# Transposes of the merged branches and of the second norm's input by DMA, as 16-bit halves, in a hybrid decoder layer

## The chip, the cores and the metric

The kernel runs on one core of one Trainium2 chip. The metric is device time in microseconds (us). The time before is the median of three runs, 1434.75 us (1433.64 to 1435.78). The kernel is written with a tile framework: buffers come from pools that hand out a buffer again when its last reader is done, a scheduler orders the instructions of each engine, and operations wrapped in `tc.keep_in_program_order` stay in the order in which the program writes them.

## The reference, cut to what matters

One layer over a sequence of 256 tokens of width 2048, all in float32:

```
h = rmsnorm(x, g_mix)
proj = h @ w_in                          # q, k, v of 16 heads, and 3 x 2048 gates
gates = sigmoid(proj[..., 3*2048:])      # one gate per branch, token and channel
o_a, o_b, o_c = three kinds of causal attention (4, 6 and 6 heads of 128)
merged = gates[0]*(o_a @ w_branch[:512]) + gates[1]*(o_b @ w_branch[512:1280])
       + gates[2]*(o_c @ w_branch[1280:])
x = x + merged @ w_out                   # "x1" below
h2 = rmsnorm(x, g_ffn)
gu = h2 @ w_gu                           # 2048 -> 2 x 5632
x = x + (silu(gu[..., :5632]) * gu[..., 5632:]) @ w_down
```

## The kernel before, in words

Every product is made of float32 operands split in two parts: `split` lets ScalarE copy an operand into a rounded high part (`hi`, type fp32r), and VectorE subtract it to get the low part (`lo`). `product` then issues three matmuls, high by high, high by low and low by high. Weights arrive as 512 KB pieces `w_raw` (two blocks of 128 rows by 512 columns, 4 buffers) through SyncE's queue, and are split into `w_hi` and `w_lo` (5 buffers each).

The activations must have the channels on the partitions. What a projection leaves is the other way round: PSUM tiles of 128 tokens by 512 columns. `transpose4` therefore lets TensorE transpose four 128x128 blocks into a PSUM tile `tr`, from which the split reads.

Two stages matter here. In the **branch stage** (about 535 to 642 us in the profile) a loop runs over four chunks of 512 columns, and within it over three branches of 4, 6 and 6 blocks of 128 rows. Each branch's product is multiplied by its gates, which GpSimd's queue loads from `gate_mem`, and added up in `ms`, one tile for each half (t = 0, 1) of the tokens. `to_m` then transposes the merged chunk into `m`, split in high and low. In the **output stage** (about 642 to 733 us) a loop over four chunks multiplies `m` by `w_out`; `keep_x1` adds x, stores the sum as `x1`, lets ScalarE sum the squares, and `next_h` makes the chunk of the next projection's input: transposed, multiplied by the norm's gain `g2` (VectorE), split, and for chunks 0 and 1 combined further (`put_sums`).

Work that follows a chunk isn't done at once. It's a generator in the list `stages`, and `project` calls `advance(stages)` once per block of 128 rows of the next projection, so that transposes and splits fall between that projection's matmuls. `finish_stages` runs what is left of the list.

The small tiles of 2 KB a partition (`half_kb`) come from the pool `scratch`, which has 12 of them for everything: merged tiles, gates, x, squares, multiplied columns.

Of the kernel before, what the change touches and what calls it, by code (L numbers as in the profile page):

```python
# [8 lines left out]

F32 = mybir.dt.float32  # L10
F32R = mybir.dt.float32r
AF = mybir.ActivationFunctionType
ALU = mybir.AluOpType
AX = mybir.AxisListType
# [3 lines left out]
P = 128  # L18
D = 2048
S = 256  # L20
NT = S // P
# [7 lines left out]
NB = 512  # L29
# [25 lines left out]
def hybrid_block(ctx: ExitStack, tc: tile.TileContext, x, g_mix, w_in, q_gain, k_gain, w_branch, w_out,  # L55
                 g_ffn, w_gu, w_down, rel_bias, onehot, extra, out):
    nc = tc.nc
# [21 lines left out]
    def pool(stack, name, side, bufs=1):  # L79
        return stack.enter_context(tc.tile_pool(name=name, bufs=bufs, side=side, reuse_waits="tile"))  # L80
# [5 lines left out]
    scratch = pool(ctx, "scratch", "right", 12)  # L86
    gx = pool(pgx, "gx", "right", 2)

    def half_kb(dt=F32):

        return scratch.tile([P, NB], dt, name="sc")
# [13 lines left out]
    def split(hi, lo, src, pin=False):  # L105
        for op in nc.scalar.copy(hi, src), nc.vector.tensor_sub(lo, src, hi.bitcast(F32)):  # L106
            if pin:
                tc.keep_in_program_order(op)

    def raw_weights(w, row0, c, col0):  # L110
        raw = wpool.tile([P, 2, NB], F32, name="w_raw", bufs=4)
        src = w[row0 + c * P: row0 + (c + 2) * P, col0: col0 + NB].rearrange("(k p) n -> p k n", p=P)
        return raw, nc.sync.dma_start(raw, src)

    def weights(w, row0, k0, nk, col0, there=()):

        for i, c in enumerate(range(k0, nk, 2)):
            raw = there[i] if i < len(there) else raw_weights(w, row0, c, col0)[0]
            hi = wpool.tile([P, 2, NB], F32R, name="w_hi")
            lo = wpool.tile([P, 2, NB], F32R, name="w_lo")  # L120
            split(hi, lo, raw)
# [4 lines left out]
    stages, slow_stages = [], []  # L126

    def advance(queue):
        while queue:
            try:  # L130
                next(queue[0])
                return
            except StopIteration:
                queue.pop(0)

    def finish_stages(queue):
        while queue:
            advance(queue)
# [25 lines left out]
    def rsqrt_mean(dst, ss, n, cols):  # L164
# [3 lines left out]
        y = small.tile([P, cols], F32, name=f"rs_y{cols}")  # L168
        nc.scalar.activation(y, v, AF.Ln)
        nc.scalar.activation(y, y, AF.Exp, scale=-0.5)  # L170
        t = small.tile([P, cols], F32, name=f"rs_t{cols}")
# [6 lines left out]
    def transpose4(src):  # L178

        pt = tr.tile([P, 4, P], F32, name="tr")  # L180
        for i in range(4):
            nc.tensor.transpose(pt[:, i, :], src[:, i * P:(i + 1) * P], ident)
        return pt


    class Columns:


        def __init__(self, pl, name, nk):
            self.hi, self.lo = (pl.tile([P, nk, S], F32R, name=f"{name}_{n}") for n in ("hi", "lo"))  # L190

# [20 lines left out]
    class Sums:  # L212
# [8 lines left out]
        def place(self, pl, c):  # L221
            self.s[c] = [pl.tile([P, 4, S], F32R, name=f"{self.name}_s{n}{c}") for n in ("hi", "lo")]

# [14 lines left out]
    class Chunks(Sums):  # L238
# [9 lines left out]
        def place(self, pl, c):  # L248
            if c in self.wc:
                super().place(pl, c)  # L250
                self.t[c] = [[pl.tile(sh, F32R, name=f"{self.name}_{t}{n}{c}") for n in ("hi", "lo")]
                             for t, sh in enumerate(([P, 4, P], [P, 2, P]))]
            else:
                self.t[c] = [pl.tile([P, 4, S], F32R, name=f"{self.name}_{n}{c}") for n in ("hi", "lo")]

# [136 lines left out]
    hs = Both(p1, h, WC)  # L392
# [6 lines left out]
    def load_x(c, queue):  # L399
        xc = [half_kb() for _ in range(NT)]  # L400
        for t in range(NT):
            queue(xc[t], x[t * P:(t + 1) * P, c * NB:(c + 1) * NB])
        return xc

    def to_h(acts, src, c, t, g, by_scalar=False):

        pt = transpose4(src)
        tmp = half_kb().rearrange("p (k q) -> p k q", k=4)
        if by_scalar:
            for i in range(4):  # L410
                nc.scalar.activation(tmp[:, i], pt[:, i], AF.Copy, scale=g[:, 4 * c + i:4 * c + i + 1])
        else:
            nc.vector.tensor_mul(tmp, pt, g[:, 4 * c:4 * c + 4, None].to_broadcast([P, 4, P]))
        acts.put(c, t, tmp)
        return tmp

    def squares(xc, dst, c, pin=False):
        for t in range(NT):
            sq = nc.scalar.activation(half_kb(), xc[t], AF.Square, accum_out=dst[:, t, c:c + 1])
            if pin:  # L420
                tc.keep_in_program_order(sq)
# [4 lines left out]
    g2 = consts.tile([P, KT], F32, name="g2")  # L426
# [4 lines left out]
    xc = [half_kb() for _ in range(NT)]  # L431
# [74 lines left out]
    with tc.manual_schedule(engines={mybir.EngineType.PE, mybir.EngineType.DVE, mybir.EngineType.Activation}):  # L506
# [14 lines left out]
        low_high(0, 1)  # L521
        high_low(0, 1)
        turned = [transpose4(xs[1][0])]
        high_high(1, 0)
        high_high(1, 1)
# [7 lines left out]
        high_high(0, 2)  # L533
        low_high(0, 2)
        turned.append(transpose4(xs[1][1]))
        high_high(1, 2)
        low_high(1, 2)
# [89 lines left out]
    def stick_breaking(hl, qT, kT, v):  # L627
# [7 lines left out]
        l = pa.tile([P, n], F32, name="p", bufs=1)  # L635
        nc.scalar.activation(l, z[:, :n], AF.Abs)
        nc.scalar.activation(l, l, AF.Exp, scale=-1.0)
        nc.scalar.activation(l, l, AF.Ln, bias=1.0)
# [214 lines left out]
    m = Columns(pool(pm, "pm", "right"), "m", KT)  # L853

    def to_m(c, srcs):
        for t in range(NT):
            m.put(c, t, transpose4(srcs[t]))
            yield

    for c in range(4):  # L860
        ms = [half_kb() for _ in range(NT)]
        for b, (k0, nk) in enumerate(((0, H_A), (H_A, H_B), (H_A + H_B, H_C))):
            gt = [half_kb() for _ in range(NT)]
            for t in range(NT):
                nc.gpsimd.dma_start(gt[t], gate_mem[b, c, t])
            ps = project(o, k0, w_branch, k0 * P, nk, c * NB)
            for t in range(NT):
                if b == 0:
                    nc.vector.tensor_mul(ms[t], ps[t], gt[t])
                else:  # L870
                    nc.vector.tensor_mul(gt[t], ps[t], gt[t])
                    nc.vector.tensor_add(ms[t], ms[t], gt[t])
        stages.append(to_m(c, ms))
    finish_stages(stages)
    ph1.close()


    pe = pool(ctx, "pe", "left")
    h2 = Chunks(pool(h2_stack, "h2p", "left"), "h", KT // 4, WC)

    def next_h(c, xc):
        hs = []
        for t in range(NT):
            hs.append(to_h(h2, xc[t], c, t, g2))
            yield
        if c in WC:
            h2.put_sums(c, *hs)
            yield
# [3 lines left out]
    def keep_x1(c, ps, xc):  # L892
        for t in range(NT):
            nc.vector.tensor_add(xc[t], ps[t], xc[t])
            nc.gpsimd.dma_start(x1[t, :, c * NB:(c + 1) * NB], xc[t])
        squares(xc, ss2, c)
        stages.append(next_h(c, xc))

    gx = pool(h2_stack, "gx2", "left", 2)
    for c in range(4):  # L900
        xc = load_x(c, nc.gpsimd.dma_start)
        ps = project(m, 0, w_out, 0, KT, c * NB)
        if c == 3:
            ahead = begin_pair(h2, w_gu, 0, D_FF)
        keep_x1(c, ps, xc)
# [191 lines left out]
```

## Time and profile before

| | |
|---|---|
| median of three runs | 1434.75 us |
| the profiled execution's own time | 1433.64 us |
| its span | 1431.9 us |
| TensorE (PE) busy | 1421.7 us, 99% |
| VectorE (DVE) busy | 1196.0 us, 84% |
| ScalarE (ACT) busy | 882.0 us, 62% |
| HBM read and written | 292.65 MB and 16.27 MB, 216 GB/s over the span |
| granted TensorE clock | 1.0 throughout |

The span is the time between the first and the last instruction; the execution's own time has 1.7 us more around it. In a row of a group, "x" is the number of instructions, then come busy time and the mean duration of one, then the idle time of that engine just before them and what ended it. A row of a timeline gives start, duration, engine, line, operation, output and input tile; in brackets the engine's idle time before it and what released it. `PEld` is the loading of the stationary operand, which overlaps the matmuls.

### The profile page before, as it was taken

To read this page: it belongs to the slowest core of one execution; us is meant where nothing else is said; L and a number is where in the kernel's file an instruction comes from. 1 tells how busy PE (TensorE), PEld (TensorE's weight loads), DVE (VectorE), ACT (ScalarE), POOL (GpSimd) and SP (SyncE) were. 2 spreads that over 40 slices of the span, in tenths; PEclk is the share of its full clock that TensorE was granted. 3 is DMA by queue.
4 is the path that set the end of the run, shared out by engine and by line. 5 is a ranking of instruction groups with operands and counts; after the bars stand their busy time and mean duration, and the time that the engine had idled before them with its cause. 6 is when DMAs were issued, how large, how long until landed. Compare 5 with 4: busy or idle time off the path is not lost. (4 is left out here: it accounts for less than half of the span.)

```text
span 1431.9 us, 17773 instructions
## 1 busy us (share of the span) xinstructions
PE 1421.7 (99%) x6404; PEld 1172.1 (82%) x6404; DVE 1196.0 (84%) x1262; ACT 882.0 (62%) x1140; POOL 72.6 (5%) x133
## 2 busy tenths in 40 slices
PE   9999999999999999999999999999999999999998
PEld 7888888888788888888888888888888888788887
DVE  7888787857999886776689999999999998886775
ACT  7667876766766665444456666666666666554453
POOL 1000000000000002100100000000000010100000
PEclk9999999999999999999999999999999999999999
DMA  8763647465666758866786657666665666767552
GB/s 270 264 218 119 220 127 247 122 221 173 215 203 238 257 194 291 278 224 211 223 299 224 224 206 251 216 225 229 219 217 191 231 212 223 256 230 240 190 169 97
DMA packets 154472, 310.09 MB, mean 217 GB/s; under 512 B 10672, under 2 KB 12288, under 8 KB 154384
## 3 DMA queue, kind: packets, MB, share of 16 engines
q1 hardware_dynamic: 143200, 275.29, 57.1%
q0 software_dynamic: 10000, 32.62, 6.5%
q10 hardware_dynamic: 1184, 1.06, 0.2%
q8 instruction: 50, 0.82, 0.2%
q14 instruction: 38, 0.31, 0.1%
HBM read 292.65 MB, written 16.27 MB: 216 GB/s over the span
## 5 line engine op out<-in xcount | busy, mean ns | idle before, releaser
L106 DVE TENSOR_TENSOR w_lo<-w_raw,w_hi 128x1024 fp32r<-128x1024 f32 x334 | 406.0, 1221 | 91.1 <-ACT w_hi L106 87.5
L106 ACT CAST w_hi<-w_raw 128x1024 fp32r<-128x1024 f32 x334 | 349.0, 1052 | 166.1 <-PE qs L162 67.4
L106 ACT CAST w_hi<-g_raw 128x1024 fp32r<-128x1024 f32 x184 | 192.6, 1053 | 120.4 <-PE ps L162 39.4
L106 DVE TENSOR_TENSOR w_lo<-g_raw,w_hi 128x1024 fp32r<-128x1024 f32 x184 | 219.6, 1220 | 36.1 <-ACT w_hi L106 35.2
L106 ACT CAST w_hi<-u 128x1024 fp32r<-128x1024 f32 x138 | 144.9, 1053 | 136.1 <-DVE u L303 65.1
L106 DVE TENSOR_TENSOR w_lo<-u,w_hi 128x1024 fp32r<-128x1024 f32 x138 | 166.5, 1221 | 37.0 <-ACT w_hi L106 35.6
L161 PE MATMUL ps<-w_lo,h_hi 128*128 128x512 f32 x360 | 140.9, 392 | 0.0
L162 PE MATMUL ps<-w_hi,h_lo 128*128 128x512 f32 x360 | 140.5, 390 | 0.0
L160 PE MATMUL ps<-w_hi,h_hi 128*128 128x512 f32 x360 | 137.5, 393 | 0.0
L161 PE MATMUL qs<-w_lo,h_hi 128*128 128x512 f32 x332 | 130.0, 392 | 0.8 <-DVE w_lo L106 0.8
L162 PE MATMUL qs<-w_hi,h_lo 128*128 128x512 f32 x332 | 129.6, 390 | 0.0
L160 PE MATMUL qs<-w_hi,h_hi 128*128 128x512 f32 x332 | 126.7, 391 | 0.0
L303 DVE TENSOR_TENSOR u<-u,g_raw 128x1024 f32<-128x1024 f32 x80 | 94.4, 1218 | 0.0
L162 PEld LDWEIGHTS ps<-w_hi,h_lo 128*128 128x128 f32 x360 | 67.6, 188 | 14.0
L161 PEld LDWEIGHTS ps<-w_lo,h_hi 128*128 128x128 f32 x360 | 67.6, 188 | 13.7
L160 PEld LDWEIGHTS ps<-w_hi,h_hi 128*128 128x128 f32 x360 | 67.5, 188 | 13.7
L161 PEld LDWEIGHTS qs<-w_lo,h_hi 128*128 128x128 f32 x332 | 62.4, 188 | 13.9 <-DVE w_lo L106 1.2
L162 PEld LDWEIGHTS qs<-w_hi,h_lo 128*128 128x128 f32 x332 | 62.4, 188 | 13.4 <-issue 0.6
L160 PEld LDWEIGHTS qs<-w_hi,h_hi 128*128 128x128 f32 x332 | 62.3, 188 | 12.7
L314 DVE TENSOR_TENSOR u<-g_raw 128x1024 f32<-128x1024 f32 x40 | 48.8, 1219 | 21.0 <-DMA g_raw<-in_w_in 16.2
L160 PE MATMUL v<-w_hi,h_hi 128*128 128x512 f32 x120 | 47.5, 396 | 0.2 <-ACT w_hi L106 0.2
L161 PE MATMUL v<-w_lo,h_hi 128*128 128x512 f32 x120 | 47.1, 393 | 0.0
(397 smaller groups left out, 2935.2 us busy)
## 6 DMA issues: line engine op xcount, KB each, us to landing
w_raw<-in_w_in SPq DMA_DIRECT2D x118, 512.0 KB, 4.6
g_raw<-in_w_gu SPq DMA_DIRECT2D x88, 512.0 KB, 5.1
w_raw<-in_w_gu SPq DMA_DIRECT2D x88, 512.0 KB, 6.4
g_raw<-in_w_in SPq DMA_DIRECT2D x72, 512.0 KB, 5.8
w_raw<-in_w_down SPq DMA_DIRECT2D x64, 512.0 KB, 4.6
w_raw<-in_w_branch SPq DMA_DIRECT2D x32, 512.0 KB, 5.1
w_raw<-in_w_out SPq DMA_DIRECT2D x32, 512.0 KB, 4.7
g_raw<-in_w_down SPq DMA_DIRECT2D x24, 512.0 KB, 5.3
```

What stands on the lines that cost most here:

```text
L106: for op in nc.scalar.copy(hi, src), nc.vector.tensor_sub(lo, src, hi.bitcast(F32)):
L160: nc.tensor.matmul(ps, ah, wh, start=start, stop=False, **how)
L161: nc.tensor.matmul(ps, ah, wl, start=False, stop=False, **how)
L162: nc.tensor.matmul(ps, al, wh, start=False, stop=stop, **how)
L303: tc.keep_in_program_order(nc.vector.tensor_add(d, d, a))
L314: nc.vector.tensor_add(d, a, b)
```

## The change

Seven times, for the four merged chunks and for chunks 0, 1 and 2 of the second norm's input, TensorE's eight transposes of a chunk go. In their place `turn_out` lets ScalarE copy a tile of 128x512 float32 into two planes of 16-bit halves (all low halves, then all high halves, 128x1024 in all), and ScalarE's queue issues a DMA transpose, which turns the eight blocks of 128x128 halves. `turn_in` lets ScalarE copy the two planes back between each other, so that the float32 words stand again, now transposed, in a scratch tile. `to_m` spreads this over the steps of the next projection: two steps to split and issue, five empty steps, two steps to join and split into high and low. In `keep_x1` the two `turn_out` come at once, and `next_h` waits four steps before it joins; the gain is then multiplied from scratch tile to scratch tile. Chunk 3 of the second norm's input stays with TensorE. The call of `finish_stages` after the loop over merged chunks goes, so that the last chunk of `m` is made during the first projection of the output stage.

```diff
+    def turn_out(src):
+        halves = scratch.tile([P, 2, NB], U16, name="sc")
+        tc.keep_in_program_order(nc.scalar.copy(halves, src.bitcast(U16).rearrange("p (n b) -> p b n", b=2)))
+        turned = scratch.tile([P, 8, P], U16, name="sc")
+        tc.keep_in_program_order(nc.scalar.dma_start_transpose(turned, halves.rearrange("p b n -> p (b n)")))
+        return turned
+
+    def turn_in(turned):
+        dst = half_kb().rearrange("p (k q) -> p k q", k=4)
+        tc.keep_in_program_order(nc.scalar.copy(dst.bitcast(U16).rearrange("p k (q b) -> p b k q", b=2),
+                                                turned.rearrange("p (b k) q -> p b k q", b=2)))
+        return dst
...
     def to_m(c, srcs):
+        turned = []
         for t in range(NT):
-            m.put(c, t, transpose4(srcs[t]))
+            turned.append(turn_out(srcs[t]))
+            yield
+        for _ in range(5):
+            yield
+        for t in range(NT):
+            m.put(c, t, turn_in(turned[t]))
             yield
...
         stages.append(to_m(c, ms))
-    finish_stages(stages)
     ph1.close()
...
-    def next_h(c, xc):
+    def next_h(c, xc, turned):
         hs = []
+        if turned:
+            for _ in range(4):
+                yield
         for t in range(NT):
-            hs.append(to_h(h2, xc[t], c, t, g2))
+            if turned:
+                tmp = turn_in(turned[t])
+                nc.vector.tensor_mul(tmp, tmp, g2[:, 4 * c:4 * c + 4, None].to_broadcast([P, 4, P]))
+                h2.put(c, t, tmp)
+            else:
+                tmp = to_h(h2, xc[t], c, t, g2)
+            hs.append(tmp)
             yield
...
-        stages.append(next_h(c, xc))
+        stages.append(next_h(c, xc, [turn_out(xc[t]) for t in range(NT)] if c < 3 else None))
```

More of the change, by code (lines that the diff above doesn't have):

```diff
@@ L11 @@
 F32R = mybir.dt.float32r
+U16 = mybir.dt.uint16
 AF = mybir.ActivationFunctionType
```

## The prediction

> **What bounds the kernel now.** I read the summary of the page first, then busy time by stretch over the two stages that the change touches (the branch projections, about 535 to 642 us, and the output projection, about 642 to 733 us), then TensorE's and ScalarE's timelines there.
>
> ```profile
> span 1431.9 us, 17773 instructions
> PE 1421.7 (99%) x6404; PEld 1172.1 (82%) x6404; DVE 1196.0 (84%) x1262; ACT 882.0 (62%) x1140; POOL 72.6 (5%) x133
> ```
>
> ```profile
> core 0: us, PE busy (x) PEld busy (x) DVE busy (x) ACT busy (x) POOL busy (x), PEclk, DMA share, GB/s
> 575.00:595.00 20.00, 20.00 (x94) 16.66 (x93) 15.63 (x20) 9.05 (x10) 3.20 (x6) 1.00 0.81 273
> 595.00:615.00 20.00, 20.00 (x94) 16.66 (x93) 15.59 (x19) 8.52 (x10) 3.22 (x6) 1.00 0.80 259
> 680.00:700.00 20.00, 20.00 (x94) 16.63 (x94) 13.80 (x17) 10.00 (x15) 2.16 (x4) 1.00 0.75 237
> 735.00:760.00 25.00, 24.84 (x113) 20.02 (x112) 23.54 (x33) 18.15 (x24) 0.00 (x0) 1.00 0.82 287
> ```
>
> TensorE has no gap in these stages, at the full granted clock; ScalarE (ACT) is busy 43 to 50% of them, VectorE (DVE) 69 to 78%, the DMA engines 75 to 81%. So in these stages a TensorE instruction that disappears is worth its slot, as long as no other engine becomes late. After 735 us PE still misses only 0.16 us of 25.
>
> The slot of a group of eight transposes is read from TensorE's timeline, and the pace of its matmuls from ScalarE's, where TensorE releases each cast of a pair of weight tiles:
>
> ```profile
> start us, us, engine line op out<-in xcount [idle before <-releaser]
> 579.94 0.39 PE L161 MATMUL qs<-w_lo,o_hi 128*128 128x512 f32 x1
> 580.16 0.39 PE L162 MATMUL qs<-w_hi,o_lo 128*128 128x512 f32 x1
> 580.40 1.03 PE L182 MATMUL tr<-ident,sc 128*128 128x128 f32 x8
> 581.18 0.48 PE L160 MATMUL qs<-w_hi,o_hi 128*128 128x512 f32 x1
> 581.50 0.40 PE L161 MATMUL qs<-w_lo,o_hi 128*128 128x512 f32 x1
> 581.73 0.39 PE L162 MATMUL qs<-w_hi,o_lo 128*128 128x512 f32 x1
> ...
> 639.71 1.05 ACT L106 CAST w_hi<-w_raw 128x1024 fp32r<-128x1024 f32 x1 [1.66 <-PE ps L162]
> 642.43 1.06 ACT L106 CAST w_hi<-w_raw 128x1024 fp32r<-128x1024 f32 x1 [1.67 <-PE ps L162]
> 645.15 1.05 ACT L106 CAST w_hi<-w_raw 128x1024 fp32r<-128x1024 f32 x1 [1.66 <-PE qs L162]
> ```
>
> **What is removed.** A pair of tiles is 12 matmuls and a cast comes every 2.72 us: a matmul's slot is 0.227 us. From the start at 580.16 to the one at 581.50 lie 1.34 us for two matmuls and eight transposes: 1.34 - 2 x 0.227 = 0.89 us for the group. The 1.03 us that the row shows overlaps with its neighbours. The change removes seven such groups, four merged chunks and three chunks of the second norm's input: 7 x 0.89 = 6.2 us of TensorE. The built program shows TensorE's order otherwise unchanged, 56 transposes fewer, so nothing else moves on this engine. The removed point at which all pending stages were finished costs nothing now, since PE shows no gap around 642 us.
>
> **What is added.** Per chunk, for each of its two row tiles: a ScalarE copy that splits 512 words into 1024 halves, a DMA transpose of 256 KB issued from ScalarE's queue, and a ScalarE copy that joins 1024 halves. VectorE's operations stay the same in number and shape; they read SBUF where they read PSUM. The nearest rows on ScalarE and VectorE:
>
> ```profile
> L106 ACT CAST w_hi<-w_raw 128x1024 fp32r<-128x1024 f32 x67 | 70.5, 1053 | 87.7 <-PE qs L162 37.1 <-PE ps L162 30.7 <-DMA w_raw<-in_w_branch 9.5
> L419 ACT ACTIVATE sc<-sc 128x512 f32<-128x512 f32 x8 | 5.0, 622 | 0.0
> L106 ACT CAST m_hi<-tr 128x512 fp32r<-128x512 f32 x8 | 4.3, 590 | 0.3
> L419 ACT ACTIVATION_READ_ACCUMULATOR sc<-sc 128x1 f32 x7 | 1.3, 186 | 0.0
> L106 ACT CAST h_shi<-sc 128x512 fp32r<-128x512 f32 x4 | 2.5, 612 | 0.0
> L106 DVE TENSOR_TENSOR w_lo<-w_raw,w_hi 128x1024 fp32r<-128x1024 f32 x68 | 83.1, 1224 | 49.5 <-ACT w_hi L106 49.5
> L872 DVE TENSOR_TENSOR sc<-sc 128x512 f32<-128x512 f32 x16 | 10.3, 683 | 0.0
> L106 DVE TENSOR_TENSOR m_lo<-tr,m_hi 128x512 fp32r<-128x512 f32 x8 | 5.1, 682 | 0.0
> ```
>
> VectorE takes 682 ns from PSUM and 683 ns from SBUF for 128x512: nothing gained or lost there. Split and join have 1024 elements, like the weight cast of 1.05 us; no row shows 2-byte elements at a stride of two. Bounds: 0.61 us (the cost by bytes, a 512-word cast) and 2 x 1.05 us if strided halves went at half rate. I take 1.05, four of them are 4.2 us a chunk.
>
> The price of issuing the transpose and its time to landing have no row of their own. The nearest:
>
> ```profile
> L1065 ACTq DMA_DIRECT2D out<-sc x8: 338/338/369, 1307.1 to 1428.6; - x8
> L113 SPq DMA_DIRECT2D w_raw<-in_w_out x32: 367/368/368, 622.9 to 710.0; - x32
> w_raw<-in_w_out SPq DMA_DIRECT2D x32, 512.0 KB, 4.7
> sc<-gate_mem POOLq DMA_DIRECT2D x24, 256.0 KB, 5.4
> a_mem<-sc POOLq DMA_DIRECT2D x22, 256.0 KB, 2.5
> x<-sc POOLq DMA_DIRECT2D x8, 256.0 KB, 7.0
> g_raw<-in_w_gu SPq DMA_DIRECT2D x8, 512.0 KB, 11.8
> ```
>
> (The last row is from the DMA view of 640 to 735 us alone, the others from the whole run.) Issue: 0.34 us is ScalarE's own row; the upper end is open, because a transpose is a different instruction, and I carry up to 3 us into the range. Landing, issue to semaphore: 2.5 us at the quiet end, 11.8 us at the crowded end. I take 5.4 to 7.0 us, the rows of equal size in the same two stages.
>
> **What hides it.** A chunk is 96 matmuls x 0.227 = 21.8 us of TensorE. ScalarE's work in a chunk of the branch stage becomes 8 casts x 1.05 + 4.2 + 2 x 0.59 + 2 x 0.34 = 14.5 us; in the output stage, with squares (2 x 0.81) and up to about 2.2 us of activation casts (two shi rows at 0.61, the others smaller), it is 8.4 + 4.2 + 0.7 + 1.6 + 2.2 = 17.1 us. Both fit into 21.8. What doesn't fit by itself is waiting: ScalarE runs in order, and the built program places split, cast A, issue 1, split, cast B, issue 2, join 1, cast C, join 2, cast D. Join 1 waits for transpose 1, and behind it stand the weight casts that feed TensorE.
>
> ```profile
> 641.94 1.28 DVE L871 TENSOR_TENSOR sc<-ps,sc 128x512 f32<-128x512 f32 x2
> 643.14 1.28 DVE L872 TENSOR_TENSOR sc<-sc 128x512 f32<-128x512 f32 x2
> ```
>
> Casts come one per 2.72 us (the timeline above), each released when TensorE frees one of five w_hi buffers; the cast's pair of weights is used four pairs, 10.9 us, later. Cast (1.05) and w_lo (1.22) take 2.3 of that, the merge on VectorE up to 2.6 more if it is in front: a cast may be 6.0 to 8.6 us late before TensorE notices. Set 0 at the end of cast A; the others would nominally begin at 1.67, 4.39 (C) and 7.11 (D). Issue 1 ends at 0.34. With landing time L, join 1 runs from L to L + 1.05, cast C follows. Transpose 2 is issued at 2.72 and lands at L + 2.72; join 2 ends at L + 3.77, the chunk's high part at L + 4.36, and only then comes cast D: late by L + 4.36 - 7.11 = L - 2.75. For 5.4 to 7.0 us that is 2.7 to 4.3 us, inside the reserve, and the next casts, with 1.67 us of idle time each, regain it before the next chunk. In the output stage squares stand ahead and two activation casts come between, which gives about the same lateness. So TensorE does not stop until L passes 8.75 to 11.35 us; I take 10. Beyond that every chunk costs L - 10, seven times.
>
> The other queues: the scratch pool's 12 tiles now serve about 14 instead of 8 requests a chunk in the branch stage. GpSimd's gate load for the last branch then takes a tile that transpose 1 has read, about 4 + L us into the chunk; with 5.4 us to land it is there by 17 us of 21.8. Behind it on GpSimd's queue stand only the next gates and x. A weight load on SyncE's queue shares its completion counter with a transpose some eight DMAs, about 20 us, earlier: free unless L is near 20 us. Transfers grow by 2 x 256 KB a chunk beside 8 x 512 KB of weights, on engines that are 75 to 81% busy; about 85 to 90% after.
>
> **The sum.** -6.2 us on TensorE, 0 for the hidden parts. The profiled execution took 1433.64 us (span 1431.9 and 1.7 around it), so it becomes 1427.4; the median of the three runs, 1434.75, becomes 1428.6, which is my forecast.
>
> **A rule against it, and one for it.** The Trainium skill, "VectorE: DVE Perf Modes", section "The three transpose paths", gives 1309 ns for a 128x128 two-byte block by DMA against 390 ns on TensorE, and advises TensorE where PSUM will do; an estimate of eight such blocks one after the other is 10.5 us of landing, and the sum by it -6.2 + 7 x 0.5 = -2.7 us. The trace's slot of 0.11 us per TensorE transpose is far under its 390. "Advanced Engine Details and Errata", section "X-Bar Transpose (TRN2)", says that transposing DMAs run as fast as plain ones, by which the sum stays -6.2; no transposing DMA is in this trace, so neither is borne out yet.
>
> **Rivals.** (1) Slower: the transposes land late. A crossbar that moves one block at a time, behind weight loads that keep the engines 75 to 81% busy, makes join 1 the wait that ends last. It decides from L = 10.9 us (7 x 0.9 = 6.2). At the crowded row's 11.8 us it costs 7 x 1.8 = 12.6, net +6.4: 1441.2; with the smaller reserve (8.75) 7 x 3.05 = 21.4, net +15: 1450. For it: 11.8 us occurs here; transpose 2 queues behind transpose 1. Against: that row is 512 KB in the most crowded 15 us. Chance 0.25.
> (2) Slower through ScalarE's own time: an issue of 3 us instead of 0.34, or strided copies at half rate (+4.2 us a chunk). In the output stage 17.1 + 5.3 + about 2.5 us of waiting is 25 us, over 21.8 by 3 for three chunks, in the branch stage 14.5 + 5.3 + 2.5 just over by 0.5 for four: +11 - 6.2 = +5, 1440. Against: both issue rows differ little, 338 and 368 ns, between 128 and 512 KB. Chance 0.15.
> (3) Most of the gain is lost: the blocks of a transpose pass one by one, and L comes to lie between the rows of 7.0 and 11.8 us just past the reserve. At 10.5 us it costs 7 x 0.5 = 3.5, net -2.7: 1432.0, within 0.2%. Chance 0.12. The skill's first rule above would end here. That TensorE's saving is not passed on at all, since VectorE's 23.5 of 25 us after 735 us sets the pace, comes here too; against it, VectorE's work starts earlier as well.
> Forecast as worked out: chance 0.48.
>
> **Numbers.** 0.2% is 2.9 us, about what three runs that spread over 2.1 us can tell. Faster 0.48, same 0.12, slower 0.40. The likeliest case alone: 1427.5 to 1431. The range goes to 1427.5 below (nothing but the 6.2 us can be gained, with 1 us of spread) and to 1456 above, past rival (1) with the small reserve; longer landings or issues are the 2 in 10 left out.
>
> **What would show it.** In the changed profile: 56 fewer transposes, TensorE busy without gaps between 535 and 730 us; the issue row on ScalarE's queue near 0.4 us; landing of the transposes 5 to 7 us; "ACT waits for DMA" rows of 1 to 4 us at the joins, and casts late by less than 6 us. Wrong if TensorE shows gaps behind w_lo or w_hi once a chunk, if the issue is over 1.5 us, or if landing is over 10 us.

## The result, and the profile after

| | before | after |
|---|---|---|
| median (lowest to highest), 6 runs each on one chip | 1434.34 us (1432.63 to 1435.78) | 1475.53 us (1474.36 to 1478.35) |
| ratio, 95% interval | | 1.0291 [1.0280, 1.0302] |
| span of the profiled execution | 1431.9 us | 1476.6 us |

The change costs 41 us where a gain of 6 was forecast: the joins wait far longer for their transposes than the prediction allowed, and TensorE runs out of weights behind them. The changed kernel's lines are numbered 1 higher up to line 184 and 16 higher behind: the split is L189, the transpose's issue L191, the join L197, the casts L107, the matmuls L161 to L163. First the page: span, engines, and the row of the granted clock.

```profile
span 1476.6 us, 17704 instructions
PE 1433.8 (97%) x6348; PEld 1175.7 (80%) x6348; DVE 1194.8 (81%) x1262; ACT 911.1 (62%) x1168; POOL 72.6 (5%) x133
PEclk9999999999999999998989999999999999999999
```

TensorE has its 56 instructions less and is busy 12 us longer: some of its matmuls ran slowly, as the granted clock below shows. The stretches that were shown of before, now:

```profile
575.00:595.00 20.00, 20.00 (x90) 16.55 (x89) 8.14 (x10) 8.03 (x9) 3.21 (x6) 1.00 1.03 206
595.00:615.00 20.00, 16.76 (x69) 13.48 (x68) 14.86 (x18) 10.36 (x11) 1.07 (x2) 0.91 0.82 210
615.00:635.00 20.00, 15.25 (x51) 11.52 (x50) 9.74 (x12) 9.57 (x10) 2.13 (x4) 0.83 0.86 209
680.00:700.00 20.00, 18.75 (x70) 15.01 (x70) 10.46 (x10) 11.46 (x15) 2.17 (x4) 0.81 0.81 224
735.00:760.00 25.00, 17.18 (x62) 13.60 (x63) 14.46 (x19) 15.34 (x20) 2.17 (x4) 0.73 0.70 180
```

Columns: length, PE, PEld, DVE, ACT, POOL busy, granted clock, DMA share, GB/s. From 575 to 595 the first two transposes are in flight: the DMA engines' share goes from 0.81 to 1.03 while the bytes fall from 273 to 206 GB/s. The gaps and the lower clock of TensorE begin in the next stretch. Issue, landing and waits of the transposes (rows of L191 and L197, and of the view of waits from 535 to 790 us):

```profile
L191 ACTq DMA_TRANSPOSE sc<-sc x14: 1248/1800/5975, 577.4 to 760.9; - x14
DMA to landing us min/median/max: 10.0/12.0/18.5
L197 ACT COPY sc<-sc x14: 1327/1348/1367, 588.6 to 772.8; 128x1024 uint16<-128x1024 uint16 x14
ACT sc L197 <- DMA sc<-sc: 64.6, 14, 14.9
POOL sc L887 <- DMA sc<-sc: 35.2, 3, 11.9
PE qs L161 <- ACT w_hi L107: 17.9, 4, 11.1
```

Every one of the fourteen joins waits, 64.6 us in all; the fourteen issues add up to 33.5 us on ScalarE. The worst place, ScalarE's timeline and then TensorE's:

```profile
721.54 1.62 ACTq L191 DMA_TRANSPOSE sc<-sc  x1
724.15 1.04 ACT L107 CAST w_hi<-w_raw 128x1024 fp32r<-128x1024 f32 x1
724.28 4.82 ACTq L191 DMA_TRANSPOSE sc<-sc  x1
740.07 1.33 ACT L197 COPY sc<-sc 128x1024 uint16<-128x1024 uint16 x1 [14.87 <-DMA sc<-sc]
741.26 1.03 ACT L107 CAST w_hi<-w_raw 128x1024 fp32r<-128x1024 f32 x1
```

```profile
730.84 0.39 PE L163 MATMUL qs<-w_hi,m_lo 128*128 128x512 f32 x1
742.35 0.79 PE L161 MATMUL qs<-w_hi,m_hi 128*128 128x512 f32 x1 [11.13 <-ACT w_hi L107]
743.61 0.79 PE L162 MATMUL qs<-w_lo,m_hi 128*128 128x512 f32 x1 [0.47 <-DVE w_lo L107]
744.20 0.63 PE L163 MATMUL qs<-w_hi,m_lo 128*128 128x512 f32 x1
744.63 0.63 PE L161 MATMUL qs<-w_hi,m_hi 128*128 128x512 f32 x1
745.05 0.63 PE L162 MATMUL qs<-w_lo,m_hi 128*128 128x512 f32 x1
```

The join stands in ScalarE's order ahead of the weight cast. It waits 14.87 us, TensorE runs out of weights and stops for 11.13 us, and then starts its matmuls every 0.43 us instead of every 0.227. Summed over all starts from 535 to 800 us, what exceeds the pace of 0.227 us is 33.8 us in gaps of over 1 us and 18.4 in shorter gaps and the slow pace (before: 0 and 1.6). 52 less before's 1.6 and the 6.2 us of removed transposes is 44: the rise of the span, 44.7.

Not every gap is a late weight. The second longest is a direct one:

```profile
678.10 0.79 PE L161 MATMUL qs<-w_hi,m_hi 128*128 128x512 f32 x1 [4.18 <-ACT m_hi L107]
```

The last merged chunk is now made during the first projection of the output stage, and TensorE itself needs it there: it waits 4.18 us for the high part of that chunk's first row tile, and 1.25 us for the second's.

### The profile page after: what moved, and what is told of

Its sections match the earlier page's. It is cut to its first block, busy times and chain, and to the rows that moved or that the text cites. A ratio compares the mean times of both kernels' runs of the same rounds, so it can differ in the third digit from the quotient of the medians.

```text
span 1476.6 us, 17704 instructions
## 1 busy us (share of the span) xinstructions
PE 1433.8 (97%) x6348; PEld 1175.7 (80%) x6348; DVE 1194.8 (81%) x1262; ACT 911.1 (62%) x1168; POOL 72.6 (5%) x133
## 5 line engine op out<-in xcount | busy, mean ns | idle before, releaser
L107 DVE TENSOR_TENSOR w_lo<-w_raw,w_hi 128x1024 fp32r<-128x1024 f32 x334 | 405.4, 1220 | 98.8 <-ACT w_hi L107 94.6
L107 ACT CAST w_hi<-w_raw 128x1024 fp32r<-128x1024 f32 x334 | 347.4, 1050 | 111.4 <-PE qs L163 41.9
L107 ACT CAST w_hi<-g_raw 128x1024 fp32r<-128x1024 f32 x184 | 192.4, 1053 | 114.2 <-PE qs L163 32.0
L107 DVE TENSOR_TENSOR w_lo<-g_raw,w_hi 128x1024 fp32r<-128x1024 f32 x184 | 219.7, 1220 | 36.8 <-ACT w_hi L107 36.0
L107 ACT CAST w_hi<-u 128x1024 fp32r<-128x1024 f32 x138 | 144.9, 1052 | 133.3 <-DVE u L319 65.0
L107 DVE TENSOR_TENSOR w_lo<-u,w_hi 128x1024 fp32r<-128x1024 f32 x138 | 166.4, 1221 | 36.3 <-ACT w_hi L107 34.9
L163 PE MATMUL ps<-w_hi,h_lo 128*128 128x512 f32 x360 | 140.4, 390 | 0.0
L161 PE MATMUL ps<-w_hi,h_hi 128*128 128x512 f32 x360 | 137.4, 392 | 0.0
L163 PE MATMUL qs<-w_hi,h_lo 128*128 128x512 f32 x332 | 129.5, 390 | 0.0
L161 PE MATMUL qs<-w_hi,h_hi 128*128 128x512 f32 x332 | 126.5, 391 | 0.0
L163 PEld LDWEIGHTS ps<-w_hi,h_lo 128*128 128x128 f32 x360 | 67.6, 188 | 14.0
L161 PEld LDWEIGHTS ps<-w_hi,h_hi 128*128 128x128 f32 x360 | 67.5, 188 | 13.7
L163 PEld LDWEIGHTS qs<-w_hi,h_lo 128*128 128x128 f32 x332 | 62.3, 188 | 13.5 <-issue 0.6
L161 PEld LDWEIGHTS qs<-w_hi,h_hi 128*128 128x128 f32 x332 | 62.3, 188 | 12.7
L197 ACT COPY sc<-sc 128x1024 uint16<-128x1024 uint16 x14 | 18.9, 1346 | 64.6 <-DMA sc<-sc 64.6
L161 PE MATMUL v<-w_hi,h_hi 128*128 128x512 f32 x120 | 47.6, 397 | 0.0
```

The lines of the kernel that those rows point to most:

```text
L161: nc.tensor.matmul(ps, ah, wh, start=start, stop=False, **how)
L163: nc.tensor.matmul(ps, al, wh, start=False, stop=stop, **how)
L197: tc.keep_in_program_order(nc.scalar.copy(dst.bitcast(U16).rearrange("p k (q b) -> p b k q", b=2), turned.rearrange("p (b k) q -> p b k q" ...
```

## The experiments

The kernel before ran beside each of them at 1433.8 to 1434.4 us.

**Is TensorE's saving real, and does ScalarE have room?** The transposes alone are taken out; splits, joins and all of VectorE's work stay.

```diff
-        turned = scratch.tile([P, 8, P], U16, name="sc")
-        ...dma_start_transpose(turned, halves...)
-        return turned
+        return halves.rearrange("p b (k q) -> p (b k) q", q=P)
```

> The changed kernel without its 14 DMA transposes: the joins read the split halves directly, so the blocks of m and of the second norm's input stay untransposed (that part of the computation is left out); splits, joins, order and the 56 missing TensorE transposes stay. Theory W (the join waits for the transpose on ScalarE's queue, and the weight casts behind it come late): with no transpose to wait for, all of the loss goes and the 6.2 us of TensorE are gained, 1428 to 1430 us. Theory A (ScalarE's own time for splits and joins, 1.05 and 1.35 us each, is too much): still slower than before by 10 us or more, 1445 or above. Theory T (the transposes' traffic delays the weights): faster as under W, 1428 to 1430, since the traffic goes as well.

Measured 1429.44 us, ratio 0.9965 [0.9952, 0.9978], with 1.2 us of gaps left. So the first half of the prediction holds: about 5 of the 6.2 us arrive, and splits and joins fit on ScalarE (theory A falls).

**What do transposes cost that nobody waits for?** First beside the unchanged work, then in the changed kernel with joins that read the halves.

```diff
 # unread: before, and in to_m and keep_x1
+            turn_out(srcs[t])
```

> TensorE transposes all chunks as before; beside that ScalarE splits the same seven chunks and issues the same 14 DMA transposes, which nobody reads, and there are no joins. Theory W: no wait, so about the time before, 1434 to 1439 us (ScalarE has room for 2 x (1.05 + 1.8) us a chunk). Theory T: the transposes occupy the DMA engines as in the changed kernel, the weights come late, and most of the 41 us stays: 1455 or above. Theory A: splits and issues are half of ScalarE's added work, 1440 to 1455.

```diff
 # unwaited: after, the transpose is issued, its result is not used
-        return turned
+        return halves.rearrange("p b (k q) -> p (b k) q", q=P)
```

> The changed kernel with all splits, all 14 DMA transposes and all joins in their places, but the joins read the split halves, not what the transposes wrote, so that no join waits (the blocks of m and of the second norm's input stay untransposed: that part of the computation is left out). Theory W (the wait of the joins on ScalarE's queue is the loss): 1432 to 1438 us, the 9 us that unread transposes cost less the 6.2 us of TensorE. Theory G (the transposes in flight hold scratch tiles, so gate loads and with them VectorE's merges come late) or T (they delay the weight loads): 1450 us or above, as with the late joins.

Unread: 1441.75 us, 1.0065 [1.0041, 1.0089], above theory W's 1439 and below theory T's 1455, in the range that stood for theory A. Unwaited: 1445.90 us, 1.0079 [1.0057, 1.0101], in neither theory's range. So 16.5 us (1445.9 - 1429.4) come from the transposes being issued and in flight, and 29.6 us (1475.5 - 1445.9) from the joins waiting. ScalarE's and TensorE's timelines of the unwaited kernel show how the first part arises:

```profile
722.49 1.05 ACT L107 CAST w_hi<-w_raw 128x1024 fp32r<-128x1024 f32 x1
723.19 6.80 ACTq L191 DMA_TRANSPOSE sc<-sc  x1
730.04 2.52 ACT L197 COPY sc<-sc 128x1024 uint16<-128x1024 uint16 x2 [6.50 <-issue]
```

```profile
733.52 0.80 PE L161 MATMUL ps<-w_hi,m_hi 128*128 128x512 f32 x1 [4.76 <-ACT w_hi L107]
```

One issue alone holds ScalarE for 6.80 us, in which the view names nothing that it waits for, and TensorE stops for 4.76. From 690 to 735 us the loads of `w_out` land in 11.7 us (median), against 4.8 in the kernel without transposes; two casts at 707.17 and 712.74 us wait 5.36 and 3.99 us for such loads, and TensorE has shorter gaps there. So both the issue and the delayed loads were suspects, and the trace shows both.

**Do the two halves of the change add up?**

> The changed kernel with the four merged chunks by DMA and all chunks of the second norm's input by TensorE. With equal shares a chunk 4/7 of 41 us, 1457 us; by the gaps in the trace (about 9 us of gaps and slow clock a chunk in the output stage, 5 in the branch stage) some 1452 us.

> The changed kernel with the four merged chunks transposed by TensorE again, so that only the three chunks of the second norm's input go by DMA (the other half of the change; merged chunks alone gave 1452.9). TensorE saves 3 x 0.89 = 2.7 us. If the two halves add up: the change as a whole lost 41 us, the merged chunks alone 18.5, which leaves 22: about 1456. If each half's loss grows with the other's (held tiles, a common clock loss): less, 1440 to 1450. By the prediction's terms (landing inside the reserve): 1432.

The edit replaces one half by `transpose4` again. Merged chunks only: 1452.88 us, 1.0132 [1.0101, 1.0163]; norm's input only: 1457.58 us, 1.0162 [1.0145, 1.0179]. 18.9 and 23.5 us over before make 42, the whole loss of 41, as the adding theory had it. Neither half is innocent.

**Would later joins and tiles of their own do?**

```diff
 # late joins: a chunk's joins come in the next chunk's to_m
+        if pending:
+            d, old = pending.pop()
+            for t in range(NT):
+                m.put(d, t, turn_in(old[t]))
+                yield
+        pending.append((c, turned))
 # own tiles
-        halves = scratch.tile([P, 2, NB], U16, name="sc")
+        halves = turns[0].tile([P, 2, NB], U16, name="halves", bufs=2)
-        turned = scratch.tile([P, 8, P], U16, name="sc")
+        turned = turns[0].tile([P, 8, P], U16, name="turned", bufs=2)
```

> The joins come a chunk later: merged chunks 0 to 2 are split and issued as in the changed kernel, but joined one chunk later (some 20 us after the issue, chunk 2 some 11 us); chunks 0 and 1 of the second norm's input likewise; merged chunk 3 and chunks 2 and 3 of the norm's input are transposed by TensorE. Theory W: five groups of transposes are saved, 5 x 0.89 = 4.4 us, and nothing waits: 1430 to 1432 us. Theory T: ten of fourteen transposes remain, so some 25 us of loss, 1455 or above.

> Merged chunks 0 to 2 alone go by DMA, split and joined in tiles of their own (8 KB a partition, none from the scratch pool), the joins five or more weight casts after the issue for chunks 0 and 1, three for chunk 2; all else is transposed by TensorE. Theory G (scratch tiles were what spoilt the late joins): 2.7 us of TensorE saved, less some 4 us for the traffic of six transposes: 1432 to 1437 us. Theory T (traffic): 1440 us or above.

Late joins in scratch tiles: 1453.74 us, 1.0146 [1.0122, 1.0170], far from theory W's 1430 to 1432. The wait moved: GpSimd's gate loads waited 39.5 us for scratch tiles that transposes were still reading or writing, and TensorE stopped for 9.3 us behind a merge without its gates. With own tiles and only merged chunks 0 to 2: 1444.08 us, 1.0063 [1.0046, 1.0081], better but still a loss, with no join waiting for a DMA. That is over theory G's 1437, so scratch tiles weren't the whole of it.

**Why does a transpose land in 12 us?** The transfers by themselves on an idle core, no layer computed, each case measured in one execution:

> No layer is computed here: one after the other, on an otherwise idle core, a DMA transpose of 256 KB, one of 128 KB, one of 32 KB, a plain DMA of 256 KB from scratch tile to scratch tile, two transposes of 256 KB issued together, four weight loads of 512 KB, four such loads with a transpose beside them, four with the plain DMA beside them. If the transpose is slow by itself, 256 KB takes 8 us or more to land on the idle core, grows with its size (about 5 us for 128 KB, 2 to 3 us for 32 KB), and the second of two lands some 6 us after the first. If it is slow only because weight loads stand in its way, it lands in 3 to 4 us alone, as the plain DMA does, and in 8 us or more beside the loads.

> The transfers by themselves, beside a stream of twelve weight loads of 512 KB (about 20 us long, longer than the four loads of the measurement before), on an otherwise idle core; the layer is left out, the time says nothing. In each step twelve loads start, and ScalarE's queue then issues: nothing; one transpose of 256 KB; one plain DMA of 256 KB in packets of 2 KB; one plain DMA of the same bytes in pieces of 256 bytes; two transposes. Theory of small packets (a queue gets its turn by packets, and a transpose of 1056 packets of some 256 bytes waits its turn behind a 2 KB packet of weights each time): the transpose lands in 9 to 13 us, the plain DMA in pieces also in 8 to 12, the plain DMA in 2 KB packets in 4 to 5, and the loads beside transpose and pieces are each some us slower. Theory of the transposing unit (it is slow beside other traffic, packets or not): the transpose takes 9 to 13 us, the pieces 4 to 5 like the plain DMA. Theory of mere crowding (any transfer waits for the loads in front): all three take 6 to 8 us. Two transposes: by the packets both land together in 14 to 20 us, by the unit the second one lands about 10 us after the first.

> The transfers by themselves on an otherwise idle core, the layer left out: a stream of twelve weight loads as before, with the extra transfer issued by SyncE after the fourth load, on the loads' own queue: one transpose of 256 KB, two transposes, 256 KB in pieces of 256 bytes, and plain 256 KB. Theory of turns by packets between queues: on the loads' queue a transfer waits for the loads in front (up to four, some 5 us) and is then served at once, so transpose, pieces and plain differ by 1 us or less, and the second of two transposes lands 1 to 1.5 us after the first (6.2 us on a queue of its own); the stream is lengthened by about 1 to 1.5 us for each transpose. If the transposes are slow in themselves beside loads: 8 us and more, and the second 5 us after the first.

Alone, 256 KB take 3.2 us transposed (issue 1.35) and 2.4 plain (issue 0.52); beside only four loads both land in about 7, when these have ended. Beside a stream of weight loads, from a queue of its own (ScalarE's), the landing rows of transposes, of plain pieces of 256 bytes (their 3.0 is one alone) and of plain rows of 2 KB:

```profile
L34 ACTq DMA_TRANSPOSE turned<-halves x3: 1286/1347/3397, 33.9 to 101.0; - x3
DMA to landing us min/median/max: 7.5/8.3/12.3
L40 ACTq DMA_DIRECT2D pieces<-halves x2: 647/679/711, 5.0 to 77.6; - x2
DMA to landing us min/median/max: 3.0/5.8/8.7
L37 ACTq DMA_DIRECT2D plain<-halves x1: 516/516/516, 56.1 to 56.1; - x1
DMA to landing us min/median/max: 5.2/5.2/5.2
```

A transpose (8.3) lands like a plain DMA in pieces of 256 bytes (8.7), not like one in whole rows (5.2): in this measurement it is the size of the packets, not the transposing. Of two issued at once the second needs 12.3 us, and its issue 3.40 instead of 1.3: the kernel's pairs, with their median of 12.0, look like this. Here the packet theory missed: it had one landing in 9 to 13 us and two together at 14 to 20, and the two landed one behind the other, 7.5 and 12.3 us after their issues. Issued on the loads' own queue (SyncE's), behind four loads:

```profile
L34 SPq DMA_TRANSPOSE turned<-halves x3: 2636/2683/4706, 35.7 to 60.3; - x3
DMA to landing us min/median/max: 6.7/7.6/8.6
L40 SPq DMA_DIRECT2D pieces<-halves x2: 639/671/703, 5.0 to 83.7; - x2
DMA to landing us min/median/max: 3.0/5.3/7.7
L37 SPq DMA_DIRECT2D plain<-halves x1: 965/965/965, 105.6 to 105.6; - x1
DMA to landing us min/median/max: 7.3/7.3/7.3
```

Transpose 7.6, pieces 7.7, whole rows (the last two lines) 7.3: there the size of packets no longer matters, and two transposes land within 1 us of each other (at 66.2 and 67.0 us of that trace). That fits queues that take turns packet by packet, as the Trainium skill has it ("DMA: Bandwidth & Descriptors", section "Queues, rings and completion order"). That on a queue of its own each small packet waits for a large one of the weights is inferred from these landings; no view shows the turns. The Trainium skill's same page, in its section "Why small descriptors are slow (HBM only)", says that transfers within SBUF don't suffer from small packets; alone that is nearly so here (3.0 us in pieces, 2.4 in rows), beside loads on another queue it isn't.

In the kernel, the same three in the place of the transposes on ScalarE's queue:

```diff
-        ...nc.scalar.dma_start_transpose(turned, halves.rearrange("p b n -> p (b n)"))
+        ...nc.scalar.dma_start(turned, <halves, whole rows>)         # plain
+        ...nc.scalar.dma_start(turned, <halves, blocks reversed>)    # pieces of 256 bytes
```

> The changed kernel with a plain DMA of the same 256 KB, scratch tile to scratch tile, from the same queue in place of each DMA transpose; joins wait for it (the blocks stay untransposed: that part of the computation is left out). If the transpose's 256-byte packets make the trouble: landing 5 to 7 us, 1428 to 1433 us. If any 256 KB on ScalarE's queue has to wait that long behind weights and gates: landing 10 us or more, 1455 us or above.

> The changed kernel with each of its fourteen transposes replaced by a plain DMA of the same 256 KB from the same queue at the same place, now moved in pieces of 256 bytes (the eight blocks are written in reversed order, and the joins read them back in that order, so they aren't transposed; the joins wait as in the change). With whole rows of 2 KB the same edit gave 1438.4, with transposes the time is 1475.5. Theory of small packets (256-byte packets take turns with the weights' 2 KB packets; pieces landed in 8.7 us beside a stream of loads, the transpose in 8.3, whole rows in 5.3): the pieces land in 10 to 13 us and the time is 1462 to 1478. Theory of the transposing unit: landing 6 to 7 us as with whole rows, 1436 to 1442.

| on ScalarE's queue, joins waiting | landing, median | issue, median | time, ratio |
|---|---|---|---|
| whole rows | 6.5 us | 0.47 us | 1438.41, 1.0031 [1.0020, 1.0042] |
| pieces of 256 bytes | 10.0 us | 0.63 us | 1452.86, 1.0135 [1.0118, 1.0151] |
| transposes (the change) | 12.0 us | 1.80 us | 1475.53, 1.0291 [1.0280, 1.0302] |

Whole rows land as the packet theory said (5 to 7 us), but they miss its time of 1428 to 1433: although no landing is over 8.8 us, the kernel is 9 us slower than without transfers (1429.4). TensorE's longest gap there, 3.59 us, stands behind a `w_lo`, just after ScalarE has waited 3.11 and 3.04 us for weight loads. The pieces land nearly as late as the transposes (the packet theory's 10 to 13 us), but the time is only 1452.9, below its 1462: small packets make 14.5 of the 37 us between rows and transposes. The other 22.7 go with what else differs, issues of 33.5 us in all against 8.9 and landing another 2 us later; the two aren't told apart here.

**Is it the queue of issue?** One word of the unwaited kernel, then of the change itself, is edited:

```diff
-        tc.keep_in_program_order(nc.scalar.dma_start_transpose(turned, ...))
+        tc.keep_in_program_order(nc.sync.dma_start_transpose(turned, ...))
```

> The kernel in which no join waits for a transpose (the joins read the halves, untransposed; 1445.9), now with the transposes issued by SyncE's queue instead of ScalarE's, among the weight loads. Theory that ScalarE is held by the issue itself (single issues of up to 6.8 us in the trace of the unwaited kernel, and a gap of 5.2 us on TensorE right behind that one): 1435 to 1440. Theory that the weight loads land late (11.7 us instead of 4.8 beside the transposes, whoever issues them): 1444 to 1450, and more if the loads now queue behind a transpose's issue on SyncE.

> The change as it stands, complete, with one edit: the fourteen transposes are issued by SyncE's queue, among the weight loads, instead of ScalarE's. Theory of the queue (on their own queue the transposes' 256-byte packets share the engines with the weights packet by packet, and their issue holds ScalarE; on the loads' queue they go in turn): landing 7 to 8 us as without the joins' wait; the prediction's own threshold was 10 us, so the joins hardly stop TensorE, and the time is 1428 to 1436. Theory of the joins (any join that waits in ScalarE's order between weight casts stops TensorE, at 7 to 8 us too): landing the same, but 1445 to 1465. Rival: the transposes queue behind weight loads that wait for their buffers, and land in over 12 us after the split: 1460 to 1475.

| transposes issued by | joins don't wait | joins wait |
|---|---|---|
| (none) | 1429.44, 0.9965 [0.9952, 0.9978] | |
| SyncE | 1428.21, 0.9966 [0.9955, 0.9977] | 1450.51, 1.0111 [1.0094, 1.0128] |
| ScalarE | 1445.90, 1.0079 [1.0057, 1.0101] | 1475.53, 1.0291 [1.0280, 1.0302] |

Unwaited and from SyncE, fourteen transposes cost nothing against none at all. That is better than the first theory's 1435 to 1440; the second theory (late loads whoever issues them) falls. How the 16.5 us divide between the issue and the late loads stays open, since this edit takes both away: ScalarE issues nothing, and from 690 to 735 us the loads of `w_out` land in 5.3 us. But "the queue alone" falls too: with the joins waiting, 1450.5 and not 1428 to 1436, in the range of the theory of the joins (1445 to 1465). The rows of the change issued by SyncE:

```profile
L191 SPq DMA_TRANSPOSE sc<-sc x14: 1237/1582/7400, 577.5 to 740.9; - x14
DMA to landing us min/median/max: 4.1/7.3/14.6
ACT sc L197 <- DMA sc<-sc: 44.8, 12, 11.5
714.13 1.33 ACT L197 COPY sc<-sc 128x1024 uint16<-128x1024 uint16 x1 [11.54 <-DMA sc<-sc]
699.78 8.81 SPq L191 DMA_TRANSPOSE sc<-sc  x2
```

The median landing is 7.3 us, under the 8.75 to 11.35 us that the prediction allowed, but the tail is not: of a pair issued without a load between them (the last row, SyncE's timeline) the first lands at 714, ScalarE stands for 11.54 us, and TensorE misses 7.5 us there. Its next longest wait, 3.0 us, follows a landing of 10.4; landings up to 10.2 us passed without such a gap. A join in ScalarE's order pays for the latest landings, not for the median.

**Both cures together.** SyncE's queue with late joins, in scratch tiles and in own tiles:

> The kernel with later joins (a chunk later; merged chunks 0 to 2 and chunks 0 and 1 of the norm's input by DMA, the rest on TensorE; 1453.7 with the issue on ScalarE), with the transposes issued by SyncE's queue. TensorE saves 5 x 0.89 = 4.5 us. Theory of the queue: 1429 to 1433. If the late joins hold scratch tiles too long for the gate loads (the gap before was behind a late gate): 1440 to 1450.

> The kernel with own tiles and later joins for merged chunks 0 to 2 only (1444.1 with the issue on ScalarE), with the transposes issued by SyncE's queue. TensorE saves 3 x 0.89 = 2.7 us. Theory of the queue: 1430 to 1433. If something else of the transposes' traffic is left: 1436 to 1444.

Five chunks, scratch tiles: 1435.88 us, 1.0012 [1.0003, 1.0022] (1453.7 with the issue on ScalarE), between the two ranges; two joins still waited 10.1 us. Merged chunks 0 to 2, own tiles: 1432.82 us, 0.9992 [0.9983, 1.0001] (1444.1 on ScalarE), and TensorE without a gap. To this, chunks of the norm's input were added, their two transposes issued a step apart and joined a chunk later:

```diff
-        if c < 0:
+        if c < 2:          # and c < 1 in the second kernel
             late.append((c, xc, []))
             stages.append(issue(late[-1]))
```

> The kernel with own tiles, joins a chunk later and the issue on SyncE for merged chunks 0 to 2 (1432.8), with chunks 0 and 1 of the second norm's input also by DMA from SyncE, their transposes issued one step apart and joined a chunk later, in scratch tiles. Five groups: TensorE saves 5 x 0.89 = 4.5 us. Theory that queue and join place were all of the loss: 1429 to 1431, faster than before. Theory that each transposed chunk keeps a cost of its own: 1433 to 1440.

> The same with chunk 0 alone of the norm's input by DMA beside the three merged chunks: four groups, 3.6 us. First theory: 1430 to 1432. Second: 1433 to 1436.

With one chunk: 1430.22 us, 0.9976 [0.9967, 0.9986], faster than before by 3.4 us (0.0024 of 1434.1) where four groups at 0.89 make 3.6. With two: 1432.92 us, 0.9991 [0.9982, 1.0000], between the first theory's 1431 and the second's 1433. Windows from 675 us on of the first, and the last of them of the second:

```profile
675.00:700.00 25.00, 25.00 (x115) 20.71 (x115) 18.03 (x25) 15.03 (x21) 2.17 (x4) 1.00 0.86 279
700.00:725.00 25.00, 25.00 (x116) 20.77 (x116) 16.61 (x22) 13.00 (x19) 2.18 (x4) 1.00 0.77 259
725.00:750.00 25.00, 24.85 (x113) 20.02 (x112) 24.26 (x34) 15.91 (x23) 1.09 (x2) 1.00 0.86 295
```

```profile
725.00:750.00 25.00, 22.12 (x99) 17.42 (x98) 24.28 (x37) 15.62 (x24) 1.09 (x2) 1.00 0.81 281
```

In the second, TensorE misses 2.9 us at the entry of the next stage, 2.1 of them waiting for `w_lo` and 0.8 for `w_hi`; that is where its further gain ends in this trace. VectorE, which makes `w_lo`, is busy 24.3 of 25 us there, but so it is in the first; why it comes late only in the second stays open.

## Why the prediction was wrong, point by point

- **TensorE's saving, 7 x 0.89 us: right.** Without the transposes' transfers the time is 1429.4 against the forecast 1428.6; TensorE has 56 transposes fewer, as said.
- **Landing: the step that failed first.** The landing time L, on which the sum's "0 for the hidden parts" rests, was taken as 5.4 to 7.0 us from plain transfers of equal size; it was 10.0 at the least, 12.0 in the median and 18.5 at the most. The rows used were plain transfers in whole rows. The range's 11.8 us end, discounted as "512 KB in the most crowded 15 us", was the typical value.
- **The formula 7 x (L - 10): wrong in kind.** At 12 us it gives 14 us, so about 1442 by rival (1); measured 1475.5. It counted one lateness per chunk from one L. Left out were the tail (a landing of 18.5), the lost clock (most of the 18.4 us, in no term of the sum), ScalarE held by the issues and late weight loads (16.5 us together, with no join waiting). Nor is nothing lost below 10 us: whole rows landed in 5.2 to 8.8 us and the time was 1438.4, 9 above the 1429.4 without transfers. Rival (1)'s direction was right; its mechanism ("a crossbar that moves one block at a time") isn't needed for most of the lateness, since plain pieces of 256 bytes land in 10.0 us.
- **The last merged chunk: left out.** Of the removed point at which all stages were finished, the prediction says only that it cost nothing before. With it gone, TensorE waits 4.18 and 1.25 us for that chunk between 673 and 682 us, a path that the prediction didn't price: it had only the weights behind the join.
- **The reserve of 6.0 to 8.6 us: too generous as used.** It allowed landings of 8.75 to 11.35 us. From SyncE's queue the median was 7.3 us, and the waiting joins still cost 22.3 us (1450.5 - 1428.2); the longest gaps of that trace follow landings of 10.4 and 14.6 us.
- **Issue, 0.34 us with 3 us as the upper end: mis-sized.** Median 1.80, up to 5.98, 33.5 us in all. The 3 us came from no row. Rival (2) priced them against ScalarE's capacity only; ScalarE as a whole stayed at 911 busy us and 33.5 of issues in 1476. In the unwaited kernel's trace one long issue of 6.80 us in front of a cast cost TensorE 4.76.
- **Split and join at 1.05 us: split right (1.05), join 1.35.** 0.6 us a chunk more, which costs nothing while the transfers are absent (1429.4).
- **Gates "by 17 of 21.8 us": wrong.** Three gate loads waited 35.2 us for scratch tiles. No wait of TensorE in that trace is put down to a merge, so it isn't shown that this cost time in the change; with late joins it did (9.3 us).
- **DMA at 85 to 90%: of little use.** With the first transposes in flight the share was 1.03 while the bytes fell, and 0.70 to 0.86 in the other stretches shown; a busy share doesn't say how much the engines move.
- **The Trainium skill's two rules.** "As fast as plain" ("Advanced Engine Details and Errata", section "X-Bar Transpose (TRN2)") is off by a third in the runs alone (3.2 and 2.4 us), true on the loads' queue (7.6 and 7.3), and not on another queue beside loads (8.3 and 5.2). 1309 ns a block ("VectorE: DVE Perf Modes", section "The three transpose paths") would, as an estimate, be 10.5 us for eight in a row; alone eight took 3.2, so the 10.0 and more in the kernel aren't blocks passing singly at that price. The same page's advice for TensorE (section "Rules for kernel authors") is borne out for the change as made, not for the last version.

## What to carry to other kernels

A DMA's price is not its landing time alone on the chip: ask which queue issues it, how large its packets are beside those of the other queues, and what stands behind its issue and behind its wait. Put small-packet transfers on the queue of the bulk loads, never two back to back, and let their result be read a chunk later, from tiles that no other queue needs. Price a wait in an in-order queue by the latest landing, not the median, and the lateness that it brings to other loads besides. These are the rules that this kernel's runs support; no other kernel was measured.

## What the hardware showed unexpectedly

- A transpose of 256 KB holds ScalarE's queue for 1.25 to 1.35 us on an idle core (two in a row 2.65), 3.40 beside a stream of loads when another is just in front, and up to 6.80 in the unwaited kernel; a plain one in whole rows takes 0.47 to 0.54 there.
- The same fourteen transfers, unwaited, cost 16.5 us from ScalarE's queue and nothing from SyncE's.
- After a gap TensorE starts matmuls every 0.43 us instead of 0.227 for some time, for example after a gap of 3.24 us:

```profile
595.87 0.39 PE L163 MATMUL ps<-w_hi,o_lo 128*128 128x512 f32 x1
599.50 0.77 PE L161 MATMUL qs<-w_hi,o_hi 128*128 128x512 f32 x1 [3.24 <-ACT w_hi L107]
601.77 0.63 PE L163 MATMUL qs<-w_hi,o_lo 128*128 128x512 f32 x1
602.20 0.47 PE L161 MATMUL qs<-w_hi,o_hi 128*128 128x512 f32 x1
602.50 0.40 PE L162 MATMUL qs<-w_lo,o_hi 128*128 128x512 f32 x1
```

The pace is back at 602.5, 3 us of work later; from 600 to 602 us the granted clock is 0.50. Shorter gaps do it too:

```profile
651.70 0.50 PE L161 MATMUL ps<-w_hi,o_hi 128*128 128x512 f32 x1 [1.05 <-ACT w_hi L107]
652.95 0.50 PE L162 MATMUL ps<-w_lo,o_hi 128*128 128x512 f32 x1 [0.76 <-DVE w_lo L107]
```

After these two, matmuls start every 0.43 us from 653.90 to 656.89, at a granted clock of 0.50 from 654 to 656 us. The Trainium skill ("TensorE: Matmul & The Clock Gate", section "Part 1: The HAM clock gate") gives about 3.4 us of idleness for the clock to halve and as much work to bring it back. The trace agrees roughly with the way back (about 3 us), not with the idleness: 1.05 and 0.76 us, one matmul apart, were enough.
